# A decoder block's input projection: X loaded once and combined in place by VectorE, a second plain quad in each half, the weights' four sums of half two on VectorE

## The chip, the cores and the metric

The program runs on one core of one Trainium2 chip. The metric is the device time of one execution, in microseconds (us). TensorE (PE in the profile) multiplies matrices, VectorE is DVE, ScalarE is ACT, GpSimd is POOL, SyncE is SP; SP, ACT and POOL can each issue DMAs.

## The reference

One layer of a decoder block on 2048 positions of width 1024, all float32. An input projection with 9216 columns feeds two branches, dilated window attention and a gated linear recurrence (RG-LRU), whose outputs are gated, projected, merged and normalised:

```python
proj = x @ w_in[l] + b_in[l]
q, k, v, g_attn, u_lru, g_lru, gate_logits = jnp.split(proj, SPLIT_POINTS, axis=-1)
...
merged = gates[:, :, 0] * y_a + gates[:, :, 1] * y_b
out = merged @ w_out[l] + b_out[l]
x = layer_norm(DEEPNORM_ALPHA * x + out, ln_gain[l], ln_bias[l])
```

The change touches the first line alone, the projection, which is the first 1500 us or so of the program. Attention and the output stages follow it.

## The kernel before, in words

**Tiles and quads.** The projection is computed transposed: 72 feature tiles of 128 columns, four chunks of 512 positions. Its work is cut into *halves* (chunks 0 and 1, then 2 and 3) and, in each half, 36 *quads*. A quad is two feature tiles by two chunks by two halves of the contraction: a 2x2 by 2x2 block product. W's blocks are A11, A12, A21, A22 (first index the feature tile), X's blocks are B11, B12, B21, B22 (first index the half of the contraction, second the chunk). A block is 128 partitions by 4 slices (`kk`) of 512; a 256 KB tile is a whole block of W, or one slice of a block of X.

**Two kinds of quad.** A *plain* quad makes its result with eight products A.B, in the order of `PLAIN`. All others use Strassen's scheme in Winograd's form (list `MID`, in the last quad of a half `EDGE`): seven products, of sums S1 to S4 of W's blocks with sums T1 to T4 of X's blocks and of some blocks themselves. Before the change quad 0 and quad 36, the first of each half, are plain.

**High and low parts.** Each operand is split in a high part (ACT copies it to a rounded type, L221 for X, L274 for W) and a low part (what is left: a subtraction, L222 for X, L233 for W, on DVE or POOL). A product is 12 matmuls, three for each slice: high by high, high by low, low by high (L613). It can't begin before the first slices of its parts are there. In half one W's low parts are stored to DRAM (`wl_scr`, L291), in half two they are loaded from there (L296) in place of being computed; a plain quad computes its own.

**The order of the work.** The program is written out product by product. The loop counts *ticks*, one for each product (`base[s]` is the tick of quad s's first product). Behind each product come the events put down for that tick (`at`), then the steps of the *chains* (rotary, silu, recurrence) that finish earlier results, as far as a budget of engine time per tick allows, and then the evacuation of the product from PSUM. Each engine works through its instructions in the order in which they were written, SP through its DMA issues too; so what is written behind a waiting instruction waits with it. Raw tiles live in 32 slots (`take`, `give`).

**X in a half.** At each half's start the four blocks are loaded (`load_raw`), split (`one_block`, low parts of alternate slices on DVE and POOL) and dropped. T1 to T4 come from a second load of the same 16 tiles (`comb_loads`, tiles named xcB), which `comb` and `fourth` add up slice by slice on DVE and split on ACT, POOL and DVE; T1 to T3 are first needed at the second product of the second quad. T4 takes the place of B12 in memory. `E0` is the tick of the first product of a half's last quad, counted so for half two's X.

**W's sums.** For a Strassen quad S1 and S3 are made by DMA: the raw block A21 is loaded twice by SP and POOL issues two accumulating DMAs on top (`added`, L251). S2 and S4 are additions (`sums`, L256); in half two S4 is on POOL.

**The program's beginning.** SP loads A11, then X; ACT issues two small loads of biases first.

Of the kernel before, what the change touches and what calls it, by code (L numbers as in the profile page):

```python
# [31 lines left out]
def hybrid_block_kernel(ctx: ExitStack, tc: tile.TileContext, a: dict, out: bass.AP):  # L32
# [36 lines left out]
    act.dma_start(b72[:, FT_V:], a["b_in"][:, FT_V:])  # L69
    pool.dma_start(b72[:, 0:FT_V], a["b_in"].rearrange("(h d) f -> d h f", h=2)[:, :, 0:FT_V])  # L70
    bh = cst.tile([P, 72], F32, name="bh")
    dve.tensor_scalar(out=bh, in0=b72, scalar1=0.5, scalar2=None, op0=ALU.mult)
    bn = cst.tile([P, 72], F32, name="bn")
    dve.tensor_scalar(out=bn, in0=b72, scalar1=-1.0, scalar2=None, op0=ALU.mult)
    lr = cst.tile([P, 8, 8], F32, name="lr")
    act.dma_start(lr, a["lru_vec"])
    brh = cst.tile([P, 2, 8], F32, name="brh")
    dve.tensor_scalar(out=brh, in0=lr[:, 5:7, :], scalar1=0.5, scalar2=None, op0=ALU.mult)
# [57 lines left out]
    PLAIN = [(fi, k, c) for c in range(2) for fi in range(2) for k in range(2)]  # L136
# [87 lines left out]
    def load_raw(b, c, kk, use=""):  # L224
        kx = kk + (4 if b[1] == "2" else 0)
        r = xr[use + b, kk] = take(f"x{use}{b}{c}{kk}", F32)
        sp.dma_start(r, a["xT"][:, kx, c * CH:(c + 1) * CH])
# [10 lines left out]
    def load_w(s, n):  # L238
        r = raw[s, n] = take(f"w{n}_{s}", F32)
        sp.dma_start(r.rearrange("p (k f) -> p k f", f=P), w_part(s, "A21" if n[0] == "S" else n))  # L240
# [27 lines left out]
    def prep_w(s, j):  # L268
# [10 lines left out]
        if plan[s][2] is None or not plan[s][0]:  # L279
            eng = pool if j % 2 == 0 else dve  # L280
# [17 lines left out]
    def units_of(s):  # L298
        return ("A11", "A12", "A21", "A22") if plan[s][2] is None else [UNIT[p] for p in plan[s][2]]
# [126 lines left out]
    dve.tensor_scalar(out=lrn, in0=lr[:, 0:4, :], scalar1=-1.0, scalar2=None, op0=ALU.mult)  # L426
# [171 lines left out]
    def product(s, j):  # L598
# [8 lines left out]
        bank = Q["b"]  # L607
# [16 lines left out]
    def evacuate(s, j):  # L624
# [3 lines left out]
        if order is None:  # L628
            fi, k, c = PLAIN[j]
            if k:  # L630
                result(s, fi, c0 + c, b, None)
# [34 lines left out]
    for s in range(1, NQ):  # L666
        t0 = base[s] - (3 if plan[s][0] else 4)
        if plan[s][2] is None:
            for d, n in ((4, "A21"), (4, "A11"), (3, "A22"), (3, "A12")):
# [20 lines left out]
    def some(kk):  # L690
        return pool if kk % 2 else dve

    def one_block(b, c, kk, eng):
        if kk == 0:
            new_block(b)
        hi_lo(b, kk, xr[b, kk], eng)
        drop_raw(b, kk)
        if eng is dve:
            spend(ACT=.66, DVE=.72)
        else:  # L700
            spend(ACT=.66, POOL=1.4)

    def comb_loads(c0, kk):
        for b, c in (("B11", c0), ("B12", c0 + 1), ("B22", c0 + 1), ("B21", c0)):
            load_raw(b, c, kk, "c")

    def comb(kk):
        r11, r12, r21, r22 = (xr["c" + b, kk] for b in ("B11", "B12", "B21", "B22"))
        if kk == 0:
            for n in ("T1", "T2", "T3"):  # L710
                new_block(n)
        tt(dve, r11, r11, r12, ALU.subtract)
        tt(dve, r12, r22, r12, ALU.subtract)
        hi_lo("T1", kk, r11, pool)
        tt(dve, r21, r11, r21, ALU.subtract)
        hi_lo("T3", kk, r12, pool)
        tt(dve, r11, r11, r22, ALU.add)
        hi_lo("T2", kk, r11, dve)
        tt(dve, r21, r21, r22, ALU.add)
        for b in ("B11", "B12", "B22"):  # L720
            drop_raw("c" + b, kk)
        spend(ACT=2.0, DVE=4.3, POOL=2.8)

    def fourth(kk):
        if kk == 0:
            new_block("T4")
        hi_lo("T4", kk, xr["cB21", kk], some(kk))
        drop_raw("cB21", kk)
        spend(ACT=.66, DVE=.36, POOL=.7)
# [3 lines left out]
    def bring(t, b, c, eng, ks=K4):  # L733

        at(t - 3, lambda: [load_raw(b, c, kk) for kk in ks])
        at(t, lambda: [one_block(b, c, kk, eng(kk)) for kk in ks])


    E0 = base[len(seq)] - 7
    bring(E0 + 2, "B11", 2, some)  # L740
    bring(E0 + 3, "B21", 2, some)
    bring(E0 + 6, "B12", 3, some)
    bring(E0 + 7, "B22", 3, some)
    for kk in K4:
        at(E0 + 6 + kk, lambda kk=kk: comb_loads(2, kk))
        at(E0 + 9 + kk, lambda kk=kk: comb(kk))
    at(E0 + 14, lambda: [fourth(kk) for kk in K4])
# [91 lines left out]

    def scales():  # L840
        softplus()
# [18 lines left out]
    for kk in K4:  # L860
        one_block("B11", 0, kk, some(kk))
    at(0, lambda: prep_w(0, 1))
    at(0, lambda: [one_block("B21", 0, kk, some(kk)) for kk in K4])
    at(0, lambda: comb_loads(0, 0))
    at(1, lambda: prep_w(0, 2))
# [526 lines left out]
```

## Time and profile before

| | |
|---|---|
| median of 3 runs | 2312.53 us (2310.76 to 2314.74) |
| the profiled execution, first to last instruction | 2307.6 us |
| TensorE, busy by the profile | 2224.6 us, 96% |
| VectorE / ScalarE / GpSimd busy | 74% / 53% / 43% |
| mean granted TensorE clock | 0.983 |

The profile gives the profiled execution's span from the first to the last instruction, 4.9 us less than the median of the runs; a time of its own beside the span isn't listed. Matmuls are pipelined, so a row's duration of one (0.39 us) is longer than the distance from one to the next; durations are counted from starts and from stretches. In a row of a timeline, the bracket at the end is the idle time just before it and what ended it. A group's row ends with the idle time before its instructions and with what released them.

### The profile page before, as it was taken

The numbers are of one execution on the slowest core, as the hardware profiler recorded it, in microseconds if no ns is written. First come the engines' busy times: TensorE is split into PE (matmuls) and PEld (weight loads), VectorE is DVE, ScalarE is ACT, GpSimd is POOL, SyncE is SP. The second block draws the span as 40 slices with busy tenths as digits, with TensorE's granted clock in tenths as the row PEclk, the third lists the DMA queues.
The fourth block names the chain that finished last, engine by engine and source line by source line (L and its number), as shares of the span: only waits on it lengthen the run. The fifth ranks groups of instructions, "written<-read, shape, count | busy, mean of one in ns | idle before, by whom it ended". The sixth has DMA issues, their size and how long they took to land.

```text
span 2307.6 us, 33976 instructions
## 1 busy us (share of the span) xinstructions
PE 2224.6 (96%) x11008; PEld 1870.4 (81%) x11008; DVE 1711.8 (74%) x3122; ACT 1215.6 (53%) x2169; POOL 991.8 (43%) x755
## 2 busy tenths in 40 slices
PE   6999999999999799999999999989999999989998
PEld 4788888888887688888888888889999878767886
DVE  6888988999998667767677877556666578747677
ACT  4457456566566466666677777456666611221100
POOL 5554645545555523223222323357676346512220
PEclk8999999999999899999999999989999999999999
DMA  7887987977977999798898888996986589864431
GB/s 243 234 241 220 266 239 210 278 221 239 276 238 227 294 257 261 213 256 236 238 240 244 257 222 244 273 251 171 246 209 159 165 262 304 268 223 161 155 119 64
DMA packets 328897, 526.24 MB, mean 228 GB/s; under 512 B 93056, under 2 KB 134032, under 8 KB 324112
## 3 DMA queue, kind: packets, MB, share of 16 engines
q1 hardware_dynamic: 289856, 464.61, 64.8%
q0 software_dynamic: 20192, 36.72, 9.6%
q10 hardware_dynamic: 18672, 22.74, 3.2%
q8 instruction: 88, 1.44, 0.3%
q14 instruction: 89, 0.73, 0.1%
HBM read 343.81 MB, written 180.16 MB: 227 GB/s over the span
## 4 chain that ended last, share of the span: by engine, by line
PE 48%; DMA 6%; issue 5%; DVE 4%; POOL 2%; ACT 2%; SPq 1%; ACTq 0%; DVEq 0%; POOLq 0%
PE q L613 30%; PE o L990 4%; PE s L951 3%; DMA A<-qh_scr 2%; PE pt L966 2%; PE z L1272 1%; PE z L1271 1%; PE z L1270 1%; PE yb L1179 1%; PE yb L1180 1%; PE yb L1178 1%; POOL me L1244 1%; DMA oc<-o_scr 1%; ACT p L957 1%; DMA atr<-at_scr 1%
## 5 line engine op out<-in xcount | busy, mean ns | idle before, releaser
L613 PE MATMUL q<-xT,hS 128*128 128x512 f32 x1680 | 525.5, 394 | 9.2 <-ACT hS L274 7.0
L613 PE MATMUL q<-xT,l 128*128 128x512 f32 x1120 | 439.6, 393 | 2.1 <-DVE l L233 2.1
L613 PE MATMUL q<-xB,hA 128*128 128x512 f32 x1248 | 390.0, 394 | 18.1 <-ACT hA L274 10.6
L613 PEld LDWEIGHTS q<-xT,hS 128*128 128x128 f32 x1680 | 318.6, 190 | 77.5 <-ACT hS L274 7.9
L613 PE MATMUL q<-xB,l 128*128 128x512 f32 x904 | 354.2, 392 | 9.3 <-POOL l L233 9.3
L613 PEld LDWEIGHTS q<-xB,hA 128*128 128x128 f32 x1248 | 235.6, 190 | 68.6 <-ACT hA L274 11.0
L613 PEld LDWEIGHTS q<-xT,l 128*128 128x128 f32 x1120 | 212.2, 189 | 47.7 <-DVE l L233 3.3
L957 ACT ACTIVATE p<-p,osb 128x256 f32<-128x256 f32 (+1 forms) x384 | 156.3, 454 | 113.5 <-DVE osb L955 111.1
L613 PEld LDWEIGHTS q<-xB,l 128*128 128x128 f32 x904 | 170.8, 189 | 46.0 <-POOL l L233 10.2
L955 DVE CUSTOM_DVE_ANT_0 p<-s,mask 128x256 f32<-128x256 f32 (+1 forms) x384 | 125.2, 363 | 96.8 <-PE s L951 56.4
L233 POOL TENSOR_TENSOR S<-S,wA 128x512 f32<-128x512 f32 x35 | 48.3, 1379 | 321.7 <-DVE S L233 209.3
L613 PE MATMUL q<-xB,hS 128*128 128x512 f32 x560 | 174.2, 392 | 1.2 <-DVE v L233 1.2
L613 PE MATMUL q<-xT,hA 128*128 128x512 f32 x560 | 173.2, 390 | 1.1 <-ACT hA L274 1.1
L251 POOL DMA_DIRECT2D wS<-in_w_in_dram x140 | 123.6, 1010 | 116.6 <-DMA wS<-in_w_in_dram 86.6
L990 PE MATMUL o<-V,ptb 128*128 128x65 f32 x1200 | 164.9, 275 | 8.4 <-ACT ptb L971 5.9
L233 POOL TENSOR_TENSOR sw<-sw,sin 128x512 f32<-128x512 f32 x96 | 154.6, 1659 | 31.7 <-ACT sw L318 22.0
L990 PEld LDWEIGHTS o<-V,ptb 128*128 128x128 f32 x1200 | 151.7, 194 | 20.3 <-ACT ptb L971 17.2
L274 ACT ACTIVATE hA<-wA 128x512 fp32r<-128x512 f32 x218 | 138.0, 635 | 23.6 <-DMA wA<-in_w_in_dram 8.8
L233 POOL TENSOR_TENSOR l<-wA,hA 128x512 fp32r<-128x512 f32 x74 | 116.7, 1577 | 69.8 <-ACT hA L274 47.7
L1244 POOL TENSOR_TENSOR me<-gA,ybr 128x512 f32<-128x512 f32 x32 | 47.8, 1507 | 188.1 <-DVE gA L1243 185.4
L613 PEld LDWEIGHTS q<-xT,hA 128*128 128x128 f32 x560 | 104.5, 188 | 23.3 <-issue 1.9
L951 PE MATMUL s<-B,A 128*128 128x256 f32 (+1 forms) x384 | 116.5, 325 | 6.6 <-POOL B L801 4.1
(196 smaller groups left out, 5093.3 us busy)
## 6 DMA issues: line engine op xcount, KB each, us to landing
wA<-in_w_in_dram SPq DMA_DIRECT2D x218, 256.0 KB, 5.7
wl_scr<-l SPq DMA_DIRECT2D x105, 512.0 KB, 4.8
l<-wl_scr SPq DMA_DIRECT2D x105, 512.0 KB, 5.5
wS<-in_w_in_dram SPq DMA_DIRECT2D x140, 256.0 KB, 4.8
wS<-in_w_in_dram POOLq DMA_DIRECT2D x140, 256.0 KB, 7.2
mg_scr<-y SPq DMA_DIRECT2D x59, 256.0 KB, 5.9
o_scr<-osb ACTq DMA_DIRECT2D x48, 264.0 KB, 6.2
oc<-o_scr SPq DMA_DIRECT2D x48, 264.0 KB, 5.2
```

Source lines behind the costliest of these rows:

```text
L233: eng.tensor_tensor(out=out, in0=in0, in1=in1, op=op)
L251: pool.dma_start(t, w_part(s, x), accum_op=ALU.add)
L274: act.activation(heads(h), heads(r, False), AF.Copy)
L613: pe.matmul(bank, w[:, ks], x[:, kk, xx], start=(first and i == 0), stop=(last and i == 11))
L951: pe.matmul(s[:, h, (0 if g == 2 and n else lo):256], q, k, start=(i == 0), stop=(i == 1))
L955: dve.tensor_tensor_reduce(out=p[:, h, lo:256], in0=s[:, h, lo:256], in1=mask[:, lo:256], scale=1.0, scalar=3e38, op0=ALU.add, op1=ALU.min ...
L957: act.activation(p[:, h, lo:256], p[:, h, lo:256], AF.Exp, scale=-1.0, bias=mm)
L966: pe.transpose(pt[:, 2 * h + x, :], p[:, h, x * P:(x + 1) * P], ident)
L990: pe.matmul(o[:, n % 2, h * 65:h * 65 + 65], ptb[:, 2 * h + x, :], V[:, kb, vo + h * 65:vo + h * 65 + 65], start=(x == lo // P), stop=(x = ...
L1178: pe.matmul(yb, WL[f][:, 0, k], xx[:, 0], start=(k == 0), stop=False)
L1179: pe.matmul(yb, WL[f][:, 0, k], xx[:, 1], start=False, stop=False)
L1244: pool.tensor_tensor(out=ME[c][:, f], in0=ga, in1=yb, op=ALU.add)
```

## The change

1. X's blocks are loaded once a half. Their raw tiles stay in their slots; sums are made in place, one T for all four slices at a time: T1 in B11, T3 in B12, T2 in B22, T4 in B21 (`block_sums`), and each is split (`sum_block`) some ticks later; `drop_block` frees the slots. DVE alone makes X's low parts.
2. Quads 1 and 37 are plain too. T2 is then first needed at the second product of quad 2 and of quad 38. The plain products' order is now by chunk, then by half of the contraction, then by feature tile, so that two PSUM banks are open at once. A plain quad's low parts of W are all made by DVE.
3. In half two S1, S2, S4 and S3 are four additions on DVE from one load of each block; the accumulating DMAs are left to half one.
4. The first loads alternate between ACT's and SP's queue; the small loads of biases go to POOL's queue, and the small operations on them go to ticks 1 and 13.

```diff
-    act.dma_start(b72[:, FT_V:], a["b_in"][:, FT_V:])
+    pool.dma_start(b72[:, FT_V:], a["b_in"][:, FT_V:])
...
-    PLAIN = [(fi, k, c) for c in range(2) for fi in range(2) for k in range(2)]
+    PLAIN = [(fi, k, c) for c in range(2) for k in range(2) for fi in range(2)]
...
     def sums(s):
         def add(n, x, y):
             t = raw[s, n] = take(f"{n}_{s}", F32)
-            tt(pool if plan[s][0] and n == "S4" else dve, t, raw[s, x], raw[s, y], ALU.add)
+            tt(dve, t, raw[s, x], raw[s, y], ALU.add)
+        if plan[s][0]:
+            add("S1", "S3", "A22")
         add("S2", "S1", "A11")
         add("S4", "S2", "A12")
         if plan[s][0]:
-            spend(DVE=.9, POOL=1.4)
+            tt(dve, raw[s, "S3"], raw[s, "S3"], raw[s, "A11"], ALU.add)
+            spend(DVE=2.6)
...
-            eng = pool if j % 2 == 0 else dve
+            eng = pool if j % 2 == 0 and plan[s][2] else dve
...
-            plan.append((h, ((f0, kind), (f1, kind)), None if p == 0 else EDGE if p == len(seq) - 1 else MID, p, kind))
+            plan.append((h, ((f0, kind), (f1, kind)), None if p < 2 else EDGE if p == len(seq) - 1 else MID, p, kind))
...
-        for d, n in ((6, "S1"), (6, "S3"), (4, "A11"), (3, "A22"), (3, "A12")):
-            at(t0 - d, lambda s=s, n=n: load_w(s, n))
-        at(t0 - 4, lambda s=s: added(s, "S1", "A22"))
-        at(t0 - 4, lambda s=s: added(s, "S3", "A11"))
+        if plan[s][0]:
+            for d, n in ((5, "A11"), (5, "S3"), (4, "A22"), (4, "A12")):
+                at(t0 - d, lambda s=s, n=n: load_w(s, n))
+        else:
+            for d, n in ((6, "S1"), (6, "S3"), (4, "A11"), (3, "A22"), (3, "A12")):
+                at(t0 - d, lambda s=s, n=n: load_w(s, n))
+            at(t0 - 4, lambda s=s: added(s, "S1", "A22"))
+            at(t0 - 4, lambda s=s: added(s, "S3", "A11"))
         at(t0 - 1, lambda s=s: sums(s))
...
+    def block_sums(n):
+        for kk in K4:
+            r11, r12, r21, r22 = (xr[b, kk] for b in ("B11", "B12", "B21", "B22"))
+            if n == "T1":
+                tt(dve, r11, r11, r12, ALU.subtract)
+            elif n == "T3":
+                tt(dve, r12, r22, r12, ALU.subtract)
+            elif n == "T2":
+                tt(dve, r22, r11, r22, ALU.add)
+            else:
+                tt(dve, r21, r22, r21, ALU.subtract)
+        spend(DVE=2.5)
...
+    def sum_events(t):
+        for d, fn, n in ((0, block_sums, "T1"), (1, block_sums, "T3"), (2, block_sums, "T2"), (3, block_sums, "T4"),
+                         (4, sum_block, "T2"), (5, sum_block, "T3"), (6, sum_block, "T1")):
+            at(t + d, lambda fn=fn, n=n: fn(n))
...
+    for d, b, c in ((2, "B11", 2), (4, "B21", 2), (7, "B12", 3), (9, "B22", 3)):
+        at(E0 + d - 3, lambda b=b, c=c: [load_raw(b, c, kk) for kk in K4])
+        at(E0 + d, lambda b=b: [one_block(b, kk) for kk in K4])
+    sum_events(E0 + 11)
+    at(E0 + 21, lambda: sum_block("T4"))
...
     load_w(0, "A11")
     for kk in K4:
-        load_raw("B11", 0, kk)
+        load_raw("B11", 0, kk, (act, sp)[kk % 2])
+    load_w(0, "A21", act)
     load_w(0, "A12")
     for kk in K4:
-        load_raw("B21", 0, kk)
-    load_w(0, "A21")
+        load_raw("B21", 0, kk, (act, sp)[kk % 2])
     load_w(0, "A22")
...
+    at(2, lambda: [one_block("B12", kk) for kk in K4])
+    at(3, lambda: [one_block("B22", kk) for kk in K4])
+    sum_events(5)
+    at(14, lambda: sum_block("T4"))
```

How this moves instructions, at two places. DVE's order near the program's beginning, behind the low parts of B22. In a name the digits behind xB or xcB are the block, the chunk and the slice. Before, one slice's sums (L233) and the split of its T2 (L222), which waits for ACT's copy:

```order
L233 TENSOR_TENSOR xcB1100_297<-xcB1100_297,xcB1210_299 128x512
L233 TENSOR_TENSOR xcB1210_299<-xcB2210_301,xcB1210_299 128x512
L233 TENSOR_TENSOR xcB2100_303<-xcB1100_297,xcB2100_303 128x512
L233 TENSOR_TENSOR xcB1100_297<-xcB1100_297,xcB2210_301 128x512
L222 TENSOR_TENSOR xT2_407<-xcB1100_297,xT2_407 128x512
L233 TENSOR_TENSOR xcB2100_303<-xcB2100_303,xcB2210_301 128x512
```

Now one T for four slices at a time, with low parts of quad 1's weights (`l0_1`) between them, and the splits of T behind all sums:

```order
L230 TENSOR_TENSOR l0_1_385<-wA11_1_300,hA11_1_383 128x512
L230 TENSOR_TENSOR xB1100_217<-xB1100_217,xB1210_239 128x512
L230 TENSOR_TENSOR xB1101_219<-xB1101_219,xB1211_241 128x512
L230 TENSOR_TENSOR xB1102_221<-xB1102_221,xB1212_243 128x512
L230 TENSOR_TENSOR xB1103_223<-xB1103_223,xB1213_245 128x512
L230 TENSOR_TENSOR l0_1_385<-wA21_1_302,hA21_1_405 128x512
L230 TENSOR_TENSOR xB1210_239<-xB2210_247,xB1210_239 128x512
```

No sum waits for another engine's copy any more. The second place is DVE in half two, at the sums of quad 40, between evacuations of quad 39 (`u39`, `v39`, and `q` for its PSUM banks). Before, S2 alone stands there:

```order
L233 TENSOR_TENSOR v39_7939<-u39_7908,q2_39_7910 128x512
L233 TENSOR_TENSOR S2_40_7956<-wS1_40_7814,wA11_40_7872 128x512
L559 SCALAR_TENSOR_TENSOR ub1_216<-q3_39_7941,bn_181,v39_7939 128x512
L233 TENSOR_TENSOR u39_7908<-u39_7908,q3_39_7941 128x512
L341 SCALAR_TENSOR_TENSOR rp8_3_7849<-rp8_3_7849,hi8_3_7979 128x512
```

Now all four do:

```order
L230 TENSOR_TENSOR v39_7818<-u39_7787,q2_39_7789 128x512
L230 TENSOR_TENSOR S1_40_7835<-wS3_40_7721,wA22_40_7755 128x512
L230 TENSOR_TENSOR S2_40_7837<-S1_40_7835,wA11_40_7719 128x512
L230 TENSOR_TENSOR S4_40_7839<-S2_40_7837,wA12_40_7757 128x512
L230 TENSOR_TENSOR wS3_40_7721<-wS3_40_7721,wA11_40_7719 128x512
L558 SCALAR_TENSOR_TENSOR ub1_212<-q3_39_7820,bn_180,v39_7818 128x512
L230 TENSOR_TENSOR u39_7787<-u39_7787,q3_39_7820 128x512
```

The evacuation of `q3` moved behind three more additions, and S4 of quad 40 has gone from POOL's order.

More of the change, by code (lines that the diff above doesn't have):

```diff
@@ L630, in evacuate @@
             if k:
-                result(s, fi, c0 + c, b, None)
+                result(s, fi, c0 + c, Q["b", fi], None)
             return
@@ L688, in hybrid_block_kernel, with one_block @@
             at(base[s] - 12, lambda i=i: start_chain(lru(i, 1, None)))
-    def some(kk):
-        return pool if kk % 2 else dve
-    def one_block(b, c, kk, eng):
+    def one_block(b, kk):
         if kk == 0:
             new_block(b)
[L696 to L729, printed above, removed]
+        hi_lo(b, kk, xr[b, kk])
+        spend(ACT=.6, DVE=.65)
+    def block_sums(n):
[10 more added lines that the diff above has]
+        spend(DVE=2.5)
```

73 lines of the change are left out of this document (35 added, 38 removed).

## The prediction

> **What bounds the kernel now.** I read the page's slices first, then a table of stretches, then who waited for whom on TensorE, then the chain of waits.
>
> ```profile
> span 2307.6 us, 33976 instructions
> PE   6999999999999799999999999989999999989998
> ```
>
> TensorE is the bound, and in the projection (some 1500 us) it has two dents: the first slice and the fifteenth (750 to 808 us). The table of stretches cuts there. Its columns are the stretch and its length, then busy time and count of PE, of weight loads, DVE, ACT and POOL, the granted clock, the DMA share and GB/s.
>
> ```profile
> 5.67:43.20 37.53, 26.64 (x98) 20.51 (x98) 23.25 (x30) 16.00 (x27) 21.00 (x17) 0.86 0.86 299
> 43.20:78.90 35.70, 26.43 (x82) 19.10 (x83) 30.74 (x52) 13.77 (x25) 16.52 (x14) 0.76 0.53 153
> 78.90:757.30 678.40, 676.83 (x3025) 558.49 (x3024) 597.67 (x706) 404.26 (x665) 358.50 (x267) 1.00 0.83 244
> 757.30:779.10 21.80, 21.80 (x97) 17.84 (x95) 13.87 (x18) 10.43 (x17) 14.07 (x11) 1.00 1.06 368
> 779.10:816.40 37.30, 23.71 (x86) 18.88 (x85) 23.34 (x28) 17.75 (x32) 14.62 (x11) 0.77 0.82 224
> 816.40:1460.00 643.60, 643.60 (x2886) 532.88 (x2885) 477.25 (x640) 448.34 (x722) 193.75 (x164) 1.00 0.86 243
> ```
>
> The fourth row is a plain quad at full clock: eight products of 12 matmuls in 21.8 us, so 2.725 us a product. Quads 0 and 1 are 15 products, worth 40.9 us. They take 5.67 to 78.93, which is 73.3, so 32.4 us are lost. Quads 36 and 37 are 15 products too and take 757.3 to 816.4, which is 59.1, so 18.2 us are lost. Between and behind these TensorE never waits. So 50.6 us can be won at most, before what the change adds.
>
> TensorE's waits at the start and at the half's change say for what:
>
> ```profile
> PE q L613 <- POOL l L233: 9.3, 2, 8.9
> PE q L613 <- ACT hS L274: 4.0, 1, 4.0
> PE q L613 <- ACT xT L221: 2.1, 1, 2.1
> ...
> PE q L613 <- ACT hA L274: 11.7, 2, 10.6
> PE q L613 <- ACT hS L274: 3.0, 1, 3.0
> ```
>
> The 8.9 us is a weight's low part that POOL makes behind two DMA issues; the others stand on ACT behind the making of T1 to T4. The chain of waits at the half's change shows that work as a relay:
>
> ```profile
> 762.83 5.62 DMA xcB<-in_xT_dram
> ...
> 768.54 0.70 DVE xcB L233
> 769.24 0.02 issue
> 769.27 0.64 ACT xT L221
> 769.91 0.07 issue
> 769.98 1.74 POOL xT L222
> 771.72 0.02 issue
> 771.75 1.77 DVE xcB L233
> ...
> 782.03 7.78 DMA l<-wl_scr
> ```
>
> A second load of X, then DVE, ACT, POOL and DVE again, some 6.8 us for each of four slices; the reload of a low part that TensorE needs stands behind it on SP's queue. The same relay in the first 80 us:
>
> ```profile
> L233 DVE TENSOR_TENSOR xcB<-xcB,xcB 128x512 f32<-128x512 f32 x20 | 19.8, 1008 | 12.1 <-POOL xT L222 11.9
> L222 POOL TENSOR_TENSOR xT<-xcB,xT 128x512 fp32r<-128x512 f32 x10 | 15.4, 1612 | 11.6 <-ACT xT L221 11.6
> L221 ACT ACTIVATE xT<-xcB 128x512 fp32r<-128x512 f32 x16 | 9.9, 629 | 27.1 <-DVE xcB L233 26.7
> ```
>
> Each engine mostly waits for the next: the relay is bound by its order, not by an engine that is full.
>
> **The change part by part.** *Two more plain quads* (1 and 37): one product more each, 2 x 2.725 = 5.45 us of TensorE on the path, unhidden. It lies in the 16 products counted below. For it T2, the first of T1 to T4 to be asked for, is due 17 products after the stage's first instead of 9.
>
> *The start.* First, what is loaded:
>
> ```profile
> 5.67 0.79 PE L613 MATMUL q<-xB,hA 128*128 128x512 f32 x1 [5.67 <-ACT xB L221]
> ...
> 12.18 0.63 PE L613 MATMUL q<-xB,hA 128*128 128x512 f32 x2
> ...
> 12.56 0.63 ACT L274 ACTIVATE hA<-wA 128x512 fp32r<-128x512 f32 x1 [0.36 <-DMA wA<-in_w_in_dram]
> ...
> 0.00:20.00 20.00, 8.40 (x26) 5.84 (x26) 11.86 (x22) 13.41 (x22) 9.34 (x15) 0.95 0.94 329
> ```
>
> Loads run at 329 GB/s with the DMA engines 94% busy, 0.80 us for a 256 KB tile; the twelfth tile is just landing at 12.56. Two issuing queues change only the order; I cost them at nothing, from -0.5 us (an earlier first tile) to +1 us (A11 shares with X). ACT now issues five loads before its first copy, about 2 us, beside the wait for A11. Twenty tiles are in by 12.6 + 8 x 0.80 = 19.0 us. The new order of the plain products needs B11 alone for two products, B21 for the next two, then B12 and B22: tiles 6, 12, 16 and 20 by products 2, 4, 6 and 8. The first product's 12 matmuls took 5.67 to 12.18, 6.5 instead of 2.7, from slow clock and waits for low parts; I keep that loss, 3.8 us. Products 3 and 4 then begin at 14.9, with tile 12 landed at 12.6; products 7 and 8 at 25.8, with tile 20 landed at 19.0. So loads hide. Quad 2 begins at 5.67 + 16 x 2.725 + 3.8 = 53.1 instead of 78.93: 25.8 us won, from 20 to 29.6 (no start loss).
>
> The clock bears on the 3.8. The Trainium skill ("TensorE: Matmul & The Clock Gate", What's actually happening) says that the array runs at half rate until one window of about 3.4 us was busy; by that alone the loss would be 1.7 us, an estimate, and the total 2.1 us lower. The trace's 3.8 holds waits as well.
>
> Does VectorE keep up, now that it makes every low part of X and of plain weights?
>
> ```profile
> 35.82 2.02 DVE L233 TENSOR_TENSOR xcB<-xcB,xcB 128x512 f32<-128x512 f32 x3
> ...
> 66.71 0.16 DVE L84 TENSOR_SCALAR spt<-lr 128x8 f32<-128x8 f32 x1
> ...
> 73.85 0.17 DVE L842 TENSOR_SCALAR sp2n<-sp 128x8 f32<-128x8 f32 x1
> ...
> 1.96 0.74 POOL L70 DMA_DIRECT2D b<-in_b_in_dram  x1
> ...
> wS<-in_w_in_dram POOLq DMA_DIRECT2D x140, 256.0 KB, 7.2
> ```
>
> Three pieces in 2.02 us: 0.67 each with no POOL in the way. Up to the low part of S2 for quad 2, VectorE makes 24 low parts of plain weights and X, 16 sums, 12 low parts of T, two weight sums and that one: 55 x 0.67 = 36.9, plus the softplus chain, 66.7 to 74.0, 7.3 us. From 6.4 that is 50.6 us, against 55.8 when TensorE asks for it (its second product of quad 2): 5 us to spare. The biases' wait for their DMA, now third in line on POOL's queue, ends by 2 + 3 x 0.74 + 7.2 = 11.4; VectorE comes there after tile 12, past 12.6. Behind it stand B12's low parts, due at 20.4. Nothing.
>
> *The half's change.* The 16 second loads go, and of each 512 KB reload one quad's worth. B11 is copied three products after its load and due five later, as before; the 20 pieces of sums and weights at products 258 to 261 take 13.4 us in 10.9 of TensorE's time, so VectorE falls 2.5 us behind, with eight products to make it up. T4 waits for B12's block to be free and then has six products. I leave 1.0 us of new waits, from 0 to 4: 59.1 - 43.6 - 1.0 = 14.5 us won.
>
> *Half two's weight sums.* Per quad VectorE gets three sums more, POOL one less, and two accumulating DMAs and one load's worth of traffic go.
>
> ```profile
> 860.00:1460.00 600.00, 448.73 (x601) 1.00 0.85 242
> L233 DVE TENSOR_TENSOR S<-wS,wA 128x512 f32<-128x512 f32 x30 | 20.5, 684 | 0.4 <-DMA wA<-in_w_in_dram 0.4
> L559 DVE SCALAR_TENSOR_TENSOR y<-q,bn,v 128x512 f32<-128x512 f32 x34 | 25.3, 745 | 22.5 <-PE q L613 22.5
> L233 POOL TENSOR_TENSOR S<-S,wA 128x512 f32<-128x512 f32 x30 | 41.5, 1382 | 284.7 <-DVE S L233 183.2 <-DMA l<-wl_scr 61.7 <-DVE vl L233 15.3
> wA<-in_w_in_dram SPq DMA_DIRECT2D x218, 256.0 KB, 5.7
> ```
>
> Thirty quads in 600 us leave VectorE 151.3 us free, 5.0 a quad; three sums are 3 x 0.684 = 2.05. What it waits for in the third row is TensorE, so it is caught up. Where half one runs (597.67 of 678.40 us busy, 88%) TensorE doesn't wait either; half two goes from 75% to 85%. The four sums stand three products (8.2 us) behind their loads, which land in 5.7. Cost: nothing, hidden by TensorE, and 34 x 2.05 = 70 us if that cover were gone.
>
> Here the row and a rule part. The Trainium skill ("SBUF — State Buffer", SBUF: two separate sides) has VectorE with two SBUF inputs and GpSimd lock each other out for a whole instruction. By it POOL's sum that goes gives VectorE up to 1.38 us back, and the three sums cost 0.67; the total stays, only the cover grows. The relay's 1.77 us pieces agree; no run here shows it for half two.
>
> Sum: 25.8 + 14.5 = 40.3. The profiled execution's span is 2307.6, and 4.9 us lie between it and the median of the runs, 2312.5, which I leave as they are (later stages are untouched and start when TensorE ends). 2307.6 - 40.3 = 2267.3 of span, 2272.2 us of time.
>
> **The rivals.** *The start is VectorE's* (0.09): its 5 us to spare are used up by waits for tiles and for ACT, and T's low parts come late by some 10 us. For: its pieces stand in one order, in which each wait delays all that follows, and they fill 44 of 47 us. Against: at 0.67 a piece it ends at 50.6. Time: 2282. *The reload stays late* (0.07): quad 38 waits for its low part's reload as quad 37 did, since cosine loads and stores stand ahead on SP's queue, at most the old 10.6 us. Against: the ACT work that held the stores is now eight products early. Time: 2283. *Half two becomes VectorE's* (0.05): the four sums in a row hold evacuations back, TensorE waits for a PSUM bank in each of 34 quads. It turns the change's sign from 40.3 / 34 = 1.2 us a quad; with the whole 2.05 us it is 2272 + 70 = 2342. Against it speaks the idle 5.0 us a quad. *The change doesn't do what it says at the start* (0.03): the loads still set the pace and quad 1 only inherits the wait; half of the 25.8 is gone, 2285.
>
> **How the numbers follow.** The forecast has 0.76. A measurement here can tell about 0.2%, 4.6 us, from no change. Low end: no start loss and no new wait, 40.3 + 3.8 + 1.0 = 45.1, so 2267.4, less 2 for the runs' spread: 2265. High end: the first two rivals and 2 us: 2285. Only the third rival can be slower: 0.04 of its 0.05, and 0.01 where it just eats the gain (within 0.2%). Faster: 0.95.
>
> **What would show it.** Right: quad 2's first matmul near 53 us and quad 38's 44 to 46 us after quad 36's; full clock from about 12 us on; no xcB load; VectorE near 85% in half two with TensorE's row still full. Wrong at the start: TensorE waits for VectorE's xT or l between 45 and 70 us. Wrong in half two: TensorE waits for S or for u, v behind 800 us. Wrong altogether: quads 2 to 35 take more than 680 us.

## The result and the profile after

The changed kernel takes 2272.94 us (median of 4 runs, 2271.11 to 2274.26), the kernel before 2311.96 us beside it (4 runs, 2310.76 to 2314.74). The ratio is 0.9827, with a 95% interval from 0.9812 to 0.9841: 39.0 us less; the forecast was 2272.2 us.

The page of the profile after, its span and TensorE's slices:

```profile
span 2270.6 us, 33643 instructions
PE   8999999999999999999999999989999999989998
```

The dent at 750 to 808 us is gone (it is the fourteenth slice; the prediction counts it as the fifteenth), and the first slice shows 8 in place of 6. The table of stretches, cut at TensorE's first matmul, the end of its slow clock, the starts of quads 2, 36 and 38, and in half two (columns as in the prediction):

```profile
0.00:8.80 8.80, 0.00 (x0) 0.00 (x0) 0.99 (x9) 2.48 (x4) 3.33 (x12) 1.00 0.77 266
8.80:13.84 5.04, 5.02 (x11) 3.65 (x12) 5.04 (x10) 5.04 (x10) 0.00 (x0) 1.00 0.99 348
13.84:55.01 41.17, 41.17 (x183) 34.05 (x182) 34.91 (x76) 22.12 (x41) 5.65 (x6) 1.00 0.61 183
55.01:733.33 678.32, 676.41 (x3025) 558.56 (x3024) 602.50 (x712) 401.43 (x661) 348.33 (x259) 1.00 0.83 243
733.33:776.85 43.52, 43.52 (x193) 36.04 (x192) 33.28 (x55) 25.88 (x46) 0.00 (x0) 1.00 0.72 216
820.00:1420.00 600.00, 599.44 (x2690) 495.95 (x2689) 481.91 (x684) 419.91 (x677) 83.69 (x58) 1.00 0.67 202
```

Quad 2 starts at 55.0 instead of 78.9 (23.9 us won), quads 2 to 35 take 678.3 as before, quads 36 and 37 take 43.5 instead of 59.1 (15.6 won). From quad 38 to attention's first matmul it is 686.9 us, 0.8 more than before. Attention starts at 1463.8 instead of 1502.6: 38.8 us won. What TensorE still waits for in the projection, up to quad 36 and from quad 38 on:

```profile
PE q L614 <- ACT xB L218: 8.8, 1, 8.8
PE q L614 <- DVE y L230: 1.4, 1, 1.4
PE q L614 <- DVE v L230: 0.3, 1, 0.3
...
PE q L614 <- DVE u L230: 0.6, 1, 0.6
```

The 8.8 us is the program's beginning: before the change the first matmul came at 5.67. The chain of waits there shows why:

```profile
0.74 5.18 DMA xB<-in_xT_dram
...
5.94 0.34 ACTq L224
...
6.31 1.28 ACT L274
...
7.60 0.63 ACT hA L274
8.23 0.53 ACT xB L218
...
8.80 0.79 PE q L614
```

ACT's last issue waits for the landing of its first load; then come the load of ACT's function table (L274, 1.28 us, hidden behind the first DMA before the change), the copy of A11 and that of X. ACT's own rows say how long its queue holds it:

```profile
0.74 0.90 ACTq L224 DMA_DIRECT2D xB<-in_xT_dram  x2
1.67 0.45 ACTq L237 DMA_DIRECT2D wA<-in_w_in_dram  x1
2.15 4.13 ACTq L224 DMA_DIRECT2D xB<-in_xT_dram  x2
```

The first issues take 0.45 us each. The last row holds two: the fourth, begun at 2.15, and the fifth, which by the chain above was issued at 5.94, just behind the landing of ACT's first load at 5.92.

### The profile page after: what moved, and what is told of

It is laid out like the page before. It is cut to its first block, busy times and chain, and to the rows that moved or that the text cites. A ratio compares the mean times of both kernels' runs of the same rounds, so it can differ in the third digit from the quotient of the medians.

```text
span 2270.6 us, 33643 instructions
## 1 busy us (share of the span) xinstructions
PE 2218.0 (98%) x11032; PEld 1869.3 (82%) x11032; DVE 1748.2 (77%) x3244; ACT 1209.9 (53%) x2161; POOL 821.6 (36%) x606
## 4 chain that ended last, share of the span: by engine, by line
PE 80%; issue 5%; DMA 5%; DVE 5%; POOL 3%; ACT 2%; SPq 1%; ACTq 0%; DVEq 0%; POOLq 0%
PE q L614 58%; PE o L988 4%; PE s L949 3%; PE yb L1177 2%; PE yb L1178 2%; PE yb L1176 2%; PE pt L964 2%; PE z L1270 1%; PE z L1269 1%; PE z L1268 1%; DMA A<-qh_scr 1%; POOL me L1242 1%; PE vtp L366 1%; DMA ybr<-yb_scr 1%; POOL C L797 1%
## 5 line engine op out<-in xcount | busy, mean ns | idle before, releaser
L614 PE MATMUL q<-xT,hS 128*128 128x512 f32 x1632 | 504.0, 390 | 1.4 <-DVE y L230 1.4
L614 PE MATMUL q<-xB,hA 128*128 128x512 f32 x1344 | 417.4, 392 | 9.5 <-ACT xB L218 8.8
L614 PE MATMUL q<-xT,l 128*128 128x512 f32 x1088 | 423.6, 389 | 0.0
L614 PE MATMUL q<-xB,l 128*128 128x512 f32 x944 | 368.4, 390 | 0.0
L614 PEld LDWEIGHTS q<-xT,hS 128*128 128x128 f32 x1632 | 305.3, 188 | 64.8 <-issue 1.8
L614 PEld LDWEIGHTS q<-xB,hA 128*128 128x128 f32 x1344 | 252.3, 189 | 62.9 <-ACT xB L218 8.8
L230 POOL TENSOR_TENSOR y<-y,h 128x512 f32<-128x512 f32 x28 | 40.3, 1440 | 413.7 <-DVE h L517 292.6
L274 ACT ACTIVATE hA<-wA 128x512 fp32r<-128x512 f32 x220 | 138.8, 635 | 21.2 <-PE g L483 6.6
L274 ACT ACTIVATE hS<-S 128x512 fp32r<-128x512 f32 x170 | 108.5, 638 | 63.8 <-DVE S L230 56.6
L230 POOL TENSOR_TENSOR l<-wA,hA 128x512 fp32r<-128x512 f32 x68 | 108.5, 1596 | 80.8 <-ACT hA L274 59.2
L614 PEld LDWEIGHTS q<-xB,hS 128*128 128x128 f32 x544 | 101.3, 188 | 21.3 <-issue 0.7
```

The costliest lines, as they stand in the source:

```text
L230: eng.tensor_tensor(out=out, in0=in0, in1=in1, op=op)
L274: act.activation(heads(h), heads(r, False), AF.Copy)
L614: pe.matmul(bank, w[:, ks], x[:, kk, xx], start=(first and i == 0), stop=(last and i == 11))
```

## Experiments

The theory: TensorE idled because a second load of X and a relay between DVE, ACT and POOL made T1 to T4; summing X in place on DVE removes both; the second plain quad gives time; half two's sums lie in VectorE's idle time; the head is late for ACT's five issues. The rivals: the second plain quad is what counts; the sums of half two have a price or a gain of their own; the two queues pay for themselves.

Two landmarks of each profiled execution tell more than the times here: TensorE's first matmul, and attention's first matmul, which ends the projection. What follows the projection is the same code in every kernel, yet took 805.0 us before, 806.8 after, and 804.2 to 815.6 in the experiments. So gains of 1 to 3 us in the projection can't be read from a median. The start varies too: with the same head the first matmul came at 7.68 to 8.80 us, and by the granted clock TensorE's slow clock lasted 3.5 to 6.4 us from there (5.0 in the changed kernel), which at half rate moves all that follows by some 0.7 us either way. From quad 38 to attention there is no such spread: six kernels with the change's row of four sums take 686.9 to 687.0 us there, the three without it 686.2.

| kernel | median (before beside it) | ratio, 95% | first matmul | attention starts | between |
|---|---|---|---|---|---|
| before | 2311.96 | 1 | 5.67 | 1502.6 | 1496.9 |
| changed | 2272.94 (2311.96) | 0.9827 (0.9812 to 0.9841) | 8.80 | 1463.8 | 1455.0 |
| first loads on one queue | 2274.97 (2312.76) | 0.9832 (0.9809 to 0.9854) | 4.94 | 1460.5 | 1455.6 |
| three loads on ACT | 2274.35 (2312.76) | 0.9829 (0.9805 to 0.9853) | 6.31 | 1462.5 | 1456.2 |
| half two's sums as before | 2274.38 (2312.76) | 0.9829 (0.9805 to 0.9854) | 8.3 | 1462.3 | 1454.0 |
| before, with plain quads 1 and 37 | 2303.53 (2312.76) | 0.9966 (0.9952 to 0.998) | 5.14 | 1493.1 | 1488.0 |
| three sums more in a row | 2312.16 (2310.9) | 1.0001 (0.9988 to 1.0013) | 8.1 | 1498.4 | 1490.3 |
| six sums more in a row | 2392.7 (2310.9) | 1.0351 (1.0335 to 1.0366) | 8.2 | 1575.2 | 1567.0 |
| X's odd low parts on GpSimd | 2273.32 (2310.9) | 0.9841 (0.9826 to 0.9855) | 8.2 | 1464.0 | 1455.8 |
| one plain quad a half | 2269.49 (2310.9) | 0.982 (0.9806 to 0.9835) | 7.68 | 1461.4 | 1453.7 |
| one sum more | 2281.02 (2311.57) | 0.9863 (0.984 to 0.9885) | 8.2 | 1465.0 | 1456.8 |
| three more, spread | 2279.95 (2311.57) | 0.9859 (0.9837 to 0.9881) | 8.2 | 1467.7 | 1459.5 |
| one plain quad, one queue | 2273.74 (2311.57) | 0.983 (0.9809 to 0.9852) | 5.39 | 1461.3 | 1455.9 |

**First loads on one queue.**

```diff
-        load_raw("B11", 0, kk, (act, sp)[kk % 2])
-    load_w(0, "A21", act)
+        load_raw("B11", 0, kk)
+    load_w(0, "A21")
...
-        load_raw("B21", 0, kk, (act, sp)[kk % 2])
+        load_raw("B21", 0, kk)
```

> The changed kernel with all first loads back on SP's queue, in the same order of tiles; the small loads of biases stay on POOL's. Theory (ACT's first work stands behind its own five issues, the last two of which hold it until 6.3 us): ACT's table load is back at about 1.7 us and hidden, the first matmul comes at 5.5 to 6.0 us in place of 8.80, the first product still loses 2.7 us to the slow clock, quad 2 starts near 52.0 in place of 55.0, and the time is about 2270 us, 3 us under the changed kernel. Rival (two queues bring the later tiles sooner, and the 3 us are their price): the first matmul is early, but TensorE then waits for tiles of B21, B12 or B22 before 30 us, quad 2 starts at 54 to 57, and the time is 2273 or more.

ACT's first rows in this run:

```profile
0.74 1.28 ACT L274 ACT_TABLE_LOAD   x1 [0.74 <-PEq L1379]
3.34 0.63 ACT L274 ACTIVATE hA<-wA 128x512 fp32r<-128x512 f32 x1 [1.31 <-DMA wA<-in_w_in_dram]
```

The table load stands ahead of the wait for A11, which lands by 3.3, and the first matmul comes at 4.94. No wait of TensorE follows before 60 us, quad 2 starts at 51.5, attention 3.3 us sooner. So the stage goes as the theory has it, and the second queue brings nothing here. The forecast of the time, 2270, is not borne out: what follows the projection took 810.9 us in this execution against 806.8, and the medians can't be told apart.

**Three loads on ACT.** Only B21's tiles go back to SP.

```diff
-        load_raw("B21", 0, kk, (act, sp)[kk % 2])
+        load_raw("B21", 0, kk)
```

> The changed kernel with three first loads on ACT's queue (two tiles of B11, and A21) in place of five; B21 comes on SP's. Theory (the fourth and fifth issue hold ACT for 4.1 us): ACT is free at about 2.1 us, its table load ends before 4, the first matmul comes at 5.5 to 6.3 us, quad 2 starts at 51.8 to 52.6, time about 2270 us. Rival (the head is late because A11 shares the DMA engines with the X tiles of a second queue, not because ACT is held): the first matmul stays at 7.5 us or later and the time within 1.5 us of 2273.

```profile
2.15 1.28 ACT L274 ACT_TABLE_LOAD   x1 [2.15 <-issue]
5.11 0.63 ACT L274 ACTIVATE hA<-wA 128x512 fp32r<-128x512 f32 x1 [1.67 <-DMA wA<-in_w_in_dram]
```

ACT is free at 2.15 and its table load hidden; quad 2 starts at 52.5. Of the late head, the two issues cost about 8.2 - 6.3 = 1.9 us (8.2 is what most runs with the changed kernel's head show; with their 7.68 to 8.80 it is 1.4 to 2.5). But A11 now lands at 5.1 instead of 3.3, with X's tiles of the second queue beside it; that is the rival's part, 6.31 - 4.94 = 1.4 us. Both were at work.

**Half two's sums as before.**

```diff
-            tt(dve, t, raw[s, x], raw[s, y], ALU.add)
-        if plan[s][0]:
-            add("S1", "S3", "A22")
+            tt(pool if plan[s][0] and n == "S4" else dve, t, raw[s, x], raw[s, y], ALU.add)
...
-            tt(dve, raw[s, "S3"], raw[s, "S3"], raw[s, "A11"], ALU.add)
```

(The loads and the two accumulating DMAs of half one hold for both halves again.)

> The changed kernel with half two's weight sums as before the change: S1 and S3 by accumulating DMAs, S2 on VectorE, S4 on GpSimd. Theory (the sums cost nothing and bring nothing, since TensorE sets the pace): VectorE's busy share between 820 and 1420 us falls from 80% to about 75%, TensorE is full there in both, time 2271 to 2274 us. Rival (the four sums on VectorE, or the traffic that they save, carry a part of the 39 us): TensorE waits in half two and the time is 2278 us or more; or, the other way, VectorE's sums had a cost and the time is 2269 us or less.

```profile
820.00:1420.00 600.00, 600.00 (x2694) 496.74 (x2693) 449.50 (x604) 421.91 (x680) 181.06 (x151) 1.00 0.85 243
```

The theory holds, though the median is 0.4 us above its range: from quad 38 to attention it takes 0.8 us less, of which 0.6 is the one wait for u. The sums bring nothing to the time and cost about that. Their price in VectorE's time can't be read from this row, since the changed kernel does fewer rotary products in the same stretch (40 `y<-y,cos` against 44). Over the whole execution the pages have VectorE busy for 1748.2 us with the sums and 1696.7 without: 51.5 us in 34 quads, 1.5 a quad.

**The second plain quads alone**, on the kernel before.

```diff
-            plan.append((h, ((f0, kind), (f1, kind)), None if p == 0 else EDGE if p == len(seq) - 1 else MID, p, kind))
+            plan.append((h, ((f0, kind), (f1, kind)), None if p < 2 else EDGE if p == len(seq) - 1 else MID, p, kind))
...
-    at(7, lambda: [fourth(kk) for kk in K4])
+    at(15, lambda: [fourth(kk) for kk in K4])
...
-    at(E0 + 14, lambda: [fourth(kk) for kk in K4])
+    at(E0 + 22, lambda: [fourth(kk) for kk in K4])
```

> The kernel before with one part of the change alone: quads 1 and 37 are plain too, and T4 is made eight products later, since it takes B12's place; X is still loaded twice, the relay of comb is as it was. Theory (part of the loss is the splitting of X itself, in quad 0, which took 37.5 us for 21.8 us of work before the change, and part is the relay, which a second plain quad gives time to end): quad 2 starts at 64 to 67 us (78.9 before, 55.0 changed), the half's change takes 44 to 50 us (59.1 before, 43.5 changed), time 2282 to 2292 us: the second plain quad alone brings 20 to 30 of the 39 us. Rival (what counts is that X is loaded once): the waits only move to quads 2 and 38, and the time stays above 2302 us.

Quad 2 starts at 69.8 us and quad 38 58.8 us after quad 36 (748.15 and 806.92), with one product more than before in each: only 9.2 us of the median are won, ratio 0.9966 (0.9952 to 0.998). My figures were wrong, and the rival's time was right, though not by its mechanism: the waits didn't move to quads 2 and 38. TensorE's longest waits up to 60 us and from quad 36 to quad 38, and ACT's rows in the first stretch:

```profile
PE q L613 <- ACT hA L274: 9.4, 3, 4.8
...
PE q L613 <- ACT hA L274: 9.8, 2, 7.4
```

```profile
34.32 0.63 ACT L221 ACTIVATE xT<-xcB 128x512 fp32r<-128x512 f32 x1 [2.86 <-DVE xcB L233]
34.85 0.61 ACT L274 ACTIVATE hA<-wA 128x512 fp32r<-128x512 f32 x1
...
42.24 0.63 ACT L221 ACTIVATE xT<-xcB 128x512 fp32r<-128x512 f32 x1 [2.88 <-DVE xcB L233]
42.78 0.61 ACT L274 ACTIVATE hA<-wA 128x512 fp32r<-128x512 f32 x1
```

The plain quad doesn't need T, but it needs the high parts of its own weights, and these stand in ACT's order behind the relay's copies, each of which waits for DVE. A quad that doesn't use the relay is still held by it. What the second plain quad did remove is the wait of 8.9 us for a low part that POOL made behind the two accumulating DMAs of quad 1: a plain quad has none, and the wait for POOL's low part is 0.6 us here.

**One plain quad a half**, X loaded once as in the change, its sums earlier.

```diff
-            plan.append((h, ((f0, kind), (f1, kind)), None if p < 2 else EDGE if p == len(seq) - 1 else MID, p, kind))
+            plan.append((h, ((f0, kind), (f1, kind)), None if p < 1 else EDGE if p == len(seq) - 1 else MID, p, kind))
...
-    at(2, lambda: [one_block("B12", kk) for kk in K4])
-    at(3, lambda: [one_block("B22", kk) for kk in K4])
-    sum_events(5)
-    at(14, lambda: sum_block("T4"))
+    at(1, lambda: [one_block("B12", kk) for kk in K4])
+    at(2, lambda: [one_block("B22", kk) for kk in K4])
+    for d, fn, n in ((3, block_sums, "T1"), (3, block_sums, "T3"), (3, block_sums, "T2"), (4, sum_block, "T2"),
+                     (5, sum_block, "T3"), (6, sum_block, "T1"), (6, block_sums, "T4"), (9, sum_block, "T4")):
+        at(d, lambda fn=fn, n=n: fn(n))
...
```

(Half two's sums and the release of X's blocks are moved in the same way.)

> The changed kernel with quads 1 and 37 in Strassen's scheme again, seven products in place of eight; X is loaded once as in the change, and its sums are put earlier: B12 and B22 are split at ticks 1 and 2, the sums of T1 to T3 stand at tick 3, their splits at ticks 4 to 6, T4 at ticks 6 and 9, and in the second half likewise eight products earlier. Theory (with X in place, VectorE has T2 split by 32 to 35 us while TensorE asks for it at 36, so the second plain quads are not needed): quad 2 starts at 52.3 to 54, the half's change (quads 36 and 37) takes 41 to 43, 3 to 5 us less in the projection than the changed kernel, 2267 to 2272 us. Rival (the second plain quad is the time that VectorE needs): TensorE waits for xT or for a low part 3 us or more at each half's start, and the time is 2274 or more.

The median is 2269.49, inside the forecast, but its interval overlaps the changed kernel's. The trace: two waits of 0.8 us for low parts in quad 1, and one of 1.1 us at the half's change; TensorE doesn't wait for T2.

```profile
35.72 0.50 PE L614 MATMUL q<-xT,l 128*128 128x512 f32 x1 [0.81 <-DVE l L230]
42.23 0.50 PE L614 MATMUL q<-xT,l 128*128 128x512 f32 x1 [0.78 <-DVE l L230]
...
739.37 0.50 PE L614 MATMUL q<-xB,l 128*128 128x512 f32 x1 [1.15 <-DVE l L230]
```

From first matmul to attention it is 1453.7 us, 1.3 less than the changed kernel. Of the 5.45 us of the two products, 1.3 remain: most of the rest goes into waits that the second plain quads had hidden, 3.4 us with one of 0.6 for y in quad 2. With X in place they are nearly neutral. The gain is there without them: it is that of X loaded once and summed in place, together with the plain quads' low parts on VectorE, which no run takes apart.

**Three and six sums more.** Both repeat S4 in the row of `sums`, three or six times, with the same result.

```diff
+            for _ in range(3):
+                tt(dve, raw[s, "S4"], raw[s, "S2"], raw[s, "A12"], ALU.add)
             tt(dve, raw[s, "S3"], raw[s, "S3"], raw[s, "A11"], ALU.add)
```

> The changed kernel with three sums more on VectorE in each of half two's 35 Strassen quads (S4 is made four times over, same result). The changed kernel left VectorE 118 us free in the 600 us from 820 to 1420, 3.9 us in each of 30 quads; three sums take about 3 x 0.70 = 2.1 us. Theory (TensorE sets the pace until VectorE is full): VectorE's busy share goes from 80% to about 90%, waits of TensorE in half two stay under 5 us, time 2272 to 2278 us. Rival (the sums stand in one row ahead of the evacuations, and it is their length in a row, not VectorE's share, that makes TensorE wait for a PSUM bank): each of the quads loses 1 us or more, 2305 us or more.

> The changed kernel with six sums more on VectorE in each of half two's 35 Strassen quads, 4.2 us against the 3.9 us that were free. Theory (TensorE sets the pace until VectorE is full, and then VectorE): VectorE's busy share is 97% or more, each quad is longer by 0.3 to 1.0 us, half two by 10 to 35 us, time 2283 to 2310 us, and TensorE's waits are for VectorE's u, v or y. Rival (work of VectorE still has slack that the busy share hides, since sums shorten when GpSimd rests): under 2279 us; rival in the other direction (ten sums in a row stop the evacuations): over 2330 us.

The theory fell. Three sums take the whole gain back, 2312.16 us, and six go to 2392.7, beyond what the theory had for either (2278 and 2310); the times of the rivals with the row hold. (Half two has 34 Strassen quads, one fewer than the expectations count.) TensorE's waits from quad 38 on, with three more, and the stretch:

```profile
PE q L616 <- DVE u L230: 16.9, 8, 5.5
PE vtp L368 <- DVE y L560: 5.6, 2, 3.8
```

```profile
820.00:1420.00 600.00, 576.32 (x2542) 471.83 (x2542) 511.46 (x730) 391.55 (x634) 82.42 (x57) 0.99 0.63 192
```

VectorE is 85% busy, and yet TensorE waits for it. For u there are eight waits, not one a quad; with the smaller groups all waits come to 24.2 us. One of them, by VectorE's rows, and then GpSimd's row at the time:

```profile
1046.03 0.68 DVE L230 TENSOR_TENSOR v<-u,q 128x512 f32<-128x512 f32 x1
1046.63 1.18 DVE L230 TENSOR_TENSOR S<-wS,wA 128x512 f32<-128x512 f32 x1
1047.85 5.54 DVE L230 TENSOR_TENSOR S<-S,wA 128x512 f32<-128x512 f32 x5
1053.31 0.69 DVE L230 TENSOR_TENSOR wS<-wS,wA 128x512 f32<-128x512 f32 x1
1053.91 0.75 DVE L560 SCALAR_TENSOR_TENSOR ub<-q,bn,v 128x512 f32<-128x512 f32 x1
1054.57 0.68 DVE L230 TENSOR_TENSOR u<-u,q 128x512 f32<-128x512 f32 x1
```

```profile
1045.52 5.15 POOL L230 TENSOR_TENSOR sw<-sw,sin 128x512 f32<-128x512 f32 x3
```

Seven sums in a row take 7.4 us here, since those beside GpSimd's rotary products take 1.2 to 1.7 us in place of 0.7. Behind them stands `u<-u,q`, which reads a PSUM bank that TensorE wants next. TensorE stands still for 3.6 us there, and then runs at a lower clock (0.96 and 0.95 in the stretches 1036.9 to 1056.9 and 1056.9 to 1076.9).

**One sum more, and three spread.** What is full: VectorE in its heavy quads, or the row ahead of the evacuation? In the spread form each of three ticks gets one instruction of the same shape, the maximum of S4 with itself.

```diff
             at(t0 + j, lambda s=s, j=j: prep_w(s, j))
+            if plan[s][0] and j < 3:
+                at(t0 + j, lambda s=s: tt(dve, raw[s, "S4"], raw[s, "S4"], raw[s, "S4"], ALU.max))
```

> The changed kernel with one sum more on VectorE in each of half two's 35 Strassen quads (S4 is made twice, same result), 0.7 us a quad. Three more cost 39 us, with VectorE at 85% on average. Theory (VectorE is full in single quads, such as the stretch from 933.7 to 953.3 us with 18.99 us busy of 19.6, so each added piece is paid in those quads): TensorE waits 2 to 10 us in half two, time 2275 to 2287 us. Rival (there is slack of one or two pieces a quad before anything is paid): waits within 1 us of the changed kernel's 0.6, time 2271 to 2275 us.

> The changed kernel with three instructions more on VectorE in each of half two's 35 Strassen quads, as in the run with three sums more, but one behind each of three products in place of all in one row (each takes the maximum of S4 with itself, same shape and result). Theory (VectorE's work in the heavy quads is what is full, wherever the three stand): about the same loss as in a row, time 2297 to 2318 us. Rival (seven sums in a row hold back the evacuation that frees a PSUM bank, and it is their length that costs): most of the 39 us is gone, time 2273 to 2285 us.

The stretch with the three spread, and its waits of TensorE from quad 38 on:

```profile
820.00:1420.00 600.00, 595.97 (x2669) 491.46 (x2668) 536.66 (x763) 414.06 (x669) 88.02 (x58) 1.00 0.67 201
```

```profile
PE q L614 <- DVE u L230: 1.9, 2, 1.6
PE q L614 <- ACT hA L274: 1.2, 1, 1.2
PE vtp L366 <- DVE y L558: 0.8, 1, 0.8
```

VectorE is busier (89%) than with three in a row (85%), and TensorE waits 3.9 us instead of 24.2. From quad 38 to attention the spread form takes 4.8 us more than the changed kernel, the row 34.7. So it is the rival: the length of the row ahead of an evacuation costs, not VectorE's share. The two differ in the operation (a maximum of one tile with itself), but hardly in what it costs VectorE: its busy time in the whole execution is 69.9 us longer with 102 spread pieces and 67.6 with 102 in the row, 0.69 and 0.66 each.

With one sum more there are two waits for u, 3.1 us in all (0.6 in the changed kernel), and 2.8 us more from quad 38 to attention. The profiled execution took 2274.5; the other three runs took 2279.7 to 2283.6, and where they lost more is not shown. The median, 2281.02, lies in the theory's range, so a slack of one more piece a quad isn't there; but the theory's reason, a VectorE that is full in single quads, doesn't fit the spread form, in which three pieces cost no more (2279.95) than this one in the row. The change's row of four is thus about the last that costs next to nothing.

**X's odd low parts on GpSimd.**

```diff
-        hi_lo(b, kk, xr[b, kk])
+        hi_lo(b, kk, xr[b, kk], pool if kk % 2 else dve)
```

> The changed kernel with the low parts of X's odd slices on GpSimd, as before the change (blocks B11 to B22 alone; T1 to T4 stay on VectorE). GpSimd took 1.4 to 1.7 us a piece where VectorE takes 0.62, and VectorE's pieces took up to 1.8 us beside it. Theory (two engines that hold each other up make a block in 4 us where VectorE alone makes it in 2.5, and TensorE asks for a block every 5.45 us): waits of 0 to 5 us in all at the start, most of them in the first two products, none at the half's change, time 2273 to 2279 us. Rival (VectorE's share of the work is what delays the start): quad 2 starts before 54.5 us and the time is 2270 or less.

2273.32 us; 0.8 us more between the landmarks, of which 0.6 is a slow clock that lasted 6.2 us in place of 5.0. The theory's low end: who makes these parts hardly matters once the relay is gone.

**One plain quad and one queue**, with the splits of T3 and T1 a tick or two later than in the run with one plain quad, so that S2's low part comes first, and T4's sums two ticks later.

> X loaded once and summed in place as in the change, one plain quad in each half (as in the run with one plain quad, with the split of T3 and T1 put a tick or two later so that S2's low part comes ahead of them), and all first loads on SP's queue. Theory (the two savings lie in different places and add up: 3.4 us at the first matmul, 2 to 4 us where the second plain quads were): first matmul at 5 to 5.5 us, second product of quad 1 delayed by less than 2 us, end of the projection at 1455 to 1459 us in place of 1463.6, time 2263 to 2270 us. Rival (a head 3.4 us earlier makes T2 late by as much, since VectorE's row up to T2 is the limit there): end of the projection at 1460 us or later, 2268 to 2273 us.

The first matmul comes at 5.39, but attention starts at 1461.3, as with two queues (1461.4). VectorE's row of X's sums, with one queue and then with two:

```profile
19.50 7.31 DVE L230 TENSOR_TENSOR xB<-xB,xB 128x512 f32<-128x512 f32 x12
...
19.40 7.31 DVE L230 TENSOR_TENSOR xB<-xB,xB 128x512 f32<-128x512 f32 x12
```

The rival holds in the main: a head that is 2.3 us earlier doesn't make VectorE's sums any earlier. TensorE doesn't wait for T2 itself, but for what stands behind it in VectorE's order (0.7 us for l, then u, v and y, 3.1 in all up to 60 us, against 2.2). That is 0.9 of the 2.3 us; another 0.8 is chance, a slow clock that lasted 5.5 us here and 3.9 there, and for the rest I have no cause. The two savings don't add up, and no kernel of these is shown to be faster than the changed one: 2273.74 (2267.6 to 2275.24).

## Why the prediction came out

- *What bounds the kernel.* Right. Both dents were waits for parts that were made late, and quads 2 to 35 didn't change (678.3 us). Most stood behind the making of T; the longest of the start, 8.9 us, was for a weight's low part on POOL behind accumulating DMAs, as the prediction says. No run parts the relay from the second load of X. By what VectorE's sums waited for, it was the relay at the start (11.9 of 12.1 us for POOL) and both at the half's change (3.5 us for POOL, 3.2 for the second load's landing).
- *Two issuing queues cost nothing* (-0.5 to +1 us; "ACT now issues five loads before its first copy, about 2 us, beside the wait for A11"). This failed, and it is the term that was most off. The five issues took until 6.3 us, the table load moved out from behind the DMA, and A11 shared its way in: the first matmul came 3.1 us later. I had read what ACT issues, and not that its own first work stands behind it.
- *The first product's loss of 3.8 us.* It was 2.6: 55.0 - 8.8 - 16 x 2.725. The slow clock, at half rate, lasted 5.0 us, to 13.84, and no wait for a low part came on top. The Trainium skill ("TensorE: Matmul & The Clock Gate", What's actually happening) has one window of about 3.4 us, by which the loss would be 1.7; the measurement lies between that and mine. The two misses leave 1.9 us: quad 2 at 55.0, forecast 53.1.
- *VectorE keeps up.* Right, with less to spare. S2's low part is done at 54.5 (forecast 50.6), asked for at 58.2: 3.7 us in place of 5. The late start and three waits for ACT (5.2 us) were longer than I had them, the pieces shorter (0.62 us).

```profile
21.09 2.50 DVE L219 TENSOR_TENSOR xB<-xB,xB 128x512 fp32r<-128x512 f32 x4 [2.89 <-ACT xB L218]
...
53.86 0.68 DVE L230 TENSOR_TENSOR l<-S,hS 128x512 fp32r<-128x512 f32 x1
```

- *The half's change.* 15.6 us won, forecast 14.5: the 1.0 us of new waits didn't come, nor did a late reload.
- *The second plain quads* were counted as they cost, 5.45 us, but their worth was taken for granted. Alone they win 9 us of the median, and with X in place they hide most of what they cost: 1.3 us remain.
- *Half two's sums cost nothing.* Right in the sum (0.8 us in the whole stretch), wrong in the reason. I took 5.0 us of idle time a quad as the cover and 85% as harmless. VectorE came to 80%, and the run with three sums more stands at 85% with the gain gone. The cover is the time until the next evacuation is due. The third rival had the mechanism ("the four sums in a row hold evacuations back") at 0.05; it was three sums away. In the changed kernel its sign, a wait for u behind 800 us, shows in one place, for 0.6 us, behind these rows:

```profile
1200.06 1.19 DVE L230 TENSOR_TENSOR S<-wS,wA 128x512 f32<-128x512 f32 x1
1201.28 3.37 DVE L230 TENSOR_TENSOR S<-S,wA 128x512 f32<-128x512 f32 x2
1204.57 0.68 DVE L230 TENSOR_TENSOR wS<-wS,wA 128x512 f32<-128x512 f32 x1
1205.17 0.74 DVE L558 SCALAR_TENSOR_TENSOR ub<-q,bn,v 128x512 f32<-128x512 f32 x1
1205.83 0.67 DVE L230 TENSOR_TENSOR u<-u,q 128x512 f32<-128x512 f32 x1
```

- *The price of the sums in VectorE's time* was 2.05 us a quad by the row and 0.67 by the Trainium skill's rule ("SBUF — State Buffer", SBUF: two separate sides), if GpSimd's sum gives time back. Measured are 1.5, between the two: the rule's direction is right, its size isn't reached. It speaks in the rows above, too: the same sums take 0.7 us alone and 1.2 to 1.7 beside GpSimd, which is busy until 1204.1 there.
- *The sum.* 40.3 forecast, 38.8 at the start of attention. The 4.9 us that I left as they are were two things: span and time of one execution lie 1.8 us apart (2270.6 and 2272.4), and the rest is that the profiled execution of before was quicker than its median. What follows the projection took 1.8 us longer in the profile after, within the spread that the experiments show there. So that forecast and median lie only 0.7 us apart is partly luck: the forecast was 1.9 us too good at the start and 0.8 in half two, 1.1 too cautious at the half's change, and the two misses at the start, 3.1 and 1.2 us, had opposite signs.

## What to carry to other kernels

Ask of an engine that is off the critical path not only how busy it is, but how long a row stands in its order ahead of what the bound engine waits for: three sums in a row cost 35 us of the projection where three spread ones, on a busier VectorE, cost 5. A quad, or any stage, that doesn't use a slow chain is still held by it if its own small step stands behind that chain in an engine's order. Before an engine is given DMA issues at the start, see what of its own stands behind them; and where the rest of the program varies by more than the gain, measure the stage by its own landmarks.

## What the runs showed of the hardware

- With four 256 KB loads under way on each of two queues, the fifth issue of each waited for a landing: ACT's came at 5.94 us, behind the landing of its first load at 5.92, and SP's at 5.75, behind that of A11 at 5.74. With all of these loads on SP's queue, six issues were begun by 3.1 us, before the first landing at 3.3. The Trainium skill ("DMA: Bandwidth & Descriptors", Issuing engines are not separate DMA queues) says that a second issuing engine saves no more than the time to initiate a DMA; here it saved nothing and cost 3.9 us at the first matmul (8.80 against 4.94).
- A tile lands later when a second queue moves others beside it: A11 was in by 3.3 us with one queue, by 5.1 with three loads on ACT's and by 5.7 with five.
- In the run with three sums more, 24.2 us of TensorE's waits became 34.7 us from quad 38 to attention: the three longest stops, of 3.6 to 5.5 us, have a lower granted clock beside them (0.83 in the stretch 1216.9 to 1236.9, which holds the wait of 5.5 us). By the granted clock that is 8.5 us.
- TensorE's slow clock at the program's start lasted 3.5 to 6.4 us from the first matmul in these thirteen profiles.
